# A two-layer hybrid diffusion step: work set into the wait for the experts' token list

## The chip, the core and the metric

The kernel runs on one core of one Trainium2 chip. The metric is the device time of one execution, in microseconds (us). The engines are TensorE (PE; its weight loads are listed apart as PEld), VectorE (DVE), ScalarE (ACT), GpSimd (POOL) and SyncE (SP), which issues most of the transfers. Each engine takes its instructions in the order of its own queue.

## The reference, cut to what matters

```python
for l in range(DEPTH):                                  # 2 layers; 128 context and 512 latent tokens
    mod = jax.nn.silu(cond) @ w_ada[l] + b_ada[l]       # w_ada: (1024, 6144); shift, scale, gate, twice
    shift1, scale1, gate1, shift2, scale2, gate2 = jnp.split(mod, 6, axis=-1)
    u = x * (1 + scale1) + shift1
    ...                                                 # attention, pooling and convolution mixers
    x = layer_norm(ALPHA * x + gate1 * mix, ln1_g, ln1_b)
    u = x * (1 + scale2) + shift2
    x = layer_norm(ALPHA * x + gate2 * expert_choice_ffn(u, ...), ln2_g, ln2_b)

def expert_choice_ffn(u, w_router, w_gate, w_up, w_down):
    cap = CAPACITY_FACTOR * T // N_EXPERTS              # 64 latent tokens, 16 context tokens an expert
    aff = jax.nn.softmax(u @ w_router, axis=-1)
    g, idx = lax.top_k(aff.swapaxes(1, 2), cap)         # each of 16 experts picks its tokens
    xs = jax.vmap(lambda ub, ib: ub[ib])(u, idx)
    hdn = jax.nn.silu(xs @ w_gate) * (xs @ w_up)        # (1024, 512) an expert
    ye = (hdn @ w_down) * g[..., None]                  # (512, 1024) an expert
    return scatter_add(idx, ye)
```

## The kernel before

Both layers run through the same code: token mixing (`token_mixing`), output projection and routing (`out_proj`), experts (`experts`). A scheduler orders each engine's instructions; `issue_after` sets one behind another, and `mm` and `turn1` (helper `inline`, L239) keep TensorE's instructions in the order in which they are written.

The experts are taken in eight pairs (`j`). A pair has 12 weight tiles of 1 MiB: gate, up and down, for two experts, in halves. `eload` puts them into a ring of 16 places, 5 in `raw` and 11 in `ex`. Places 0 to 11 hold the first pair. Place 12 takes a gate tile of the second pair early; the loads of places 13 to 15 (`GATE`) are held behind a 1x1 memset on POOL which follows the first gather, so that these loads don't meet that gather.

The latent tokens' list comes last before the experts: eight rounds of `topk` on VectorE, some small operations (`route_lat`), a transpose on TensorE (`tcol` of `ldup`, into `ps_tc`), casts to indices (`lgi`). With `lgi`, POOL gathers the first pair's rows (`xsl` from `zrow`); TensorE transposes them (`tr`) and starts the first pair's gate product, `ps_g`. A second transpose (`lvd`) brings the list's weights `lg`.

While the list is made, TensorE does the first pair's context products (`fill`, into `ps_gc`). The rest of the context work of that pair stands behind the list: silu on ACT (`sc`) and product on VectorE (`hc`, L1165), transposes (`ps_hcT`), copy (`hcT`), down products (`ps_dc`, 16 matmuls, which the trace counts as 32), scaling (`yc`), and two scatters on POOL into `yaccc`. Each later pair runs its half latent products, its context products (8 steps `k`), the other half, and the down products.

The modulation `mod` is 6 groups of 2048 columns over the two layers, each in eight blocks (`ada_load`, `ada_compute`: 1 MiB of weights and 4 matmuls a block, L185). The blocks of the second layer's group 1 are the late ones of the first layer: `tick()` sets them among the value projection and the first attention heads. POOL also does the residual rows: `xa` times `ln_g`, plus `ln_b`, then a store into `yacc` (`residual`).

## Time and profile before

| | |
|---|---|
| three runs, median | 1258.03 us (1255.51 to 1258.26) |
| profiled execution, its own time | 1255.77 us |
| its span, first to last instruction | 1254.0 us |
| busy share of the span | PE 94%, PEld 56%, DVE 42%, ACT 29%, POOL 20% |
| bytes moved | 342.34 MB, 273 GB/s over the span |
| first layer: list transposed, first gate product | 361.20 us, 372.38 us |
| second layer: the same | 948.77 us, 959.72 us |

The profiled execution is one of those at the lower end: its own time is 2.26 us under the median. Times inside it are counted from the span's start. A matmul of these weights stands as two records in the trace.

### The profile page before, as it was taken

The numbers are of one execution on the slowest core, as the hardware profiler recorded it, in microseconds if no ns is written. First come the engines' busy times: TensorE is split into PE (matmuls) and PEld (weight loads), VectorE is DVE, ScalarE is ACT, GpSimd is POOL, SyncE is SP. The second block draws the span as 40 slices with busy tenths as digits, with TensorE's granted clock in tenths as the row PEclk, the third lists the DMA queues.
The fourth block names the chain that finished last, engine by engine and source line by source line (L and its number), as shares of the span: only waits on it lengthen the run. The fifth ranks groups of instructions, "written<-read, shape, count | busy, mean of one in ns | idle before, by whom it ended". The sixth has DMA issues, their size and how long they took to land.

```text
span 1254.0 us, 18189 instructions
## 1 busy us (share of the span) xinstructions
PE 1178.4 (94%) x7244; PEld 707.5 (56%) x7244; DVE 523.4 (42%) x1237; ACT 367.8 (29%) x805; POOL 254.6 (20%) x237
## 2 busy tenths in 40 slices
PE   5999999999959999999999999999996999999994
PEld 1887786987723333333359998698762333333331
DVE  1455454775551121111165766477744111111126
ACT  1542234673321111111065324476341111111111
POOL 0210001003341111113134600200334121112304
PEclk8899999999979999999999999999998999999997
DMA  9958674344869999999951414616396999999972
GB/s 366 323 199 318 218 270 168 136 153 148 300 243 405 397 404 400 407 413 373 339 162 66 131 56 201 220 51 221 134 356 234 403 395 406 409 408 400 351 253 84
DMA packets 85077, 342.34 MB, mean 273 GB/s; under 512 B 18712, under 2 KB 32088, under 8 KB 54400
## 3 DMA queue, kind: packets, MB, share of 16 engines
q1 hardware_dynamic: 73568, 305.96, 62.8%
q0 software_dynamic: 9840, 29.45, 8.6%
q10 hardware_dynamic: 1584, 5.77, 1.1%
q8 instruction: 57, 0.93, 0.3%
q14 instruction: 28, 0.23, 0.1%
HBM read 313.73 MB, written 27.51 MB: 272 GB/s over the span
## 4 chain that ended last, share of the span: by engine, by line
PE 85%; DVE 6%; ACT 3%; DMA 2%; issue 2%; POOL 1%; SPq 1%; POOLq 0%; ACTq 0%; DVEq 0%
PE ps_d L239 9%; PE ps_g L239 9%; PE ps_u L239 9%; PE ps_gc L239 8%; PE ps_dc L239 4%; PE ps_ada L185 4%; PE ps_c L230 3%; PE ps_o L230 3%; PE ps_o L231 3%; PE ps_o L232 3%; PE ps_c L231 3%; PE ps_c L232 3%; PE tr L239 1%; PE ps_p L732 1%; PE ps_a L230 1%
## 5 line engine op out<-in xcount | busy, mean ns | idle before, releaser
L239 PE MATMUL ps_d<-wd,hT 128*64 128x512 f32 x512 | 114.4, 596 | 4.8 <-DVE yc L1186 3.2
L239 PE MATMUL ps_g<-wg,xT 128*64 128x512 f32 x512 | 116.1, 595 | 0.1
L239 PE MATMUL ps_u<-wu,xT 128*64 128x512 f32 x512 | 115.4, 592 | 0.0
L239 PE MATMUL ps_gc<-wu,xc 128*32 128x512 f32 x512 | 115.0, 594 | 0.0
L239 PE MATMUL ps_gc<-wg,xc 128*32 128x512 f32 x512 | 115.0, 594 | 0.0
L1163 ACT ACTIVATE sc<-ps_gc 32x512 f32<-32x512 f32 x32 | 18.8, 588 | 304.7 <-PE ps_gc L239 276.3
L1165 DVE TENSOR_TENSOR hc<-ps_gc,sc 32x512 f32<-32x512 f32 x32 | 22.0, 687 | 175.0 <-ACT sc L1163 174.9
L239 PEld LDWEIGHTS ps_d<-wd,hT 128*64 128x64 f32 x512 | 37.0, 137 | 80.2 <-issue 76.1
L239 PEld LDWEIGHTS ps_g<-wg,xT 128*64 128x64 f32 x512 | 36.0, 137 | 75.2 <-issue 70.1
L239 PEld LDWEIGHTS ps_u<-wu,xT 128*64 128x64 f32 x512 | 37.2, 137 | 72.6 <-issue 72.6
L239 PEld LDWEIGHTS ps_gc<-wg,xc 128*32 128x32 f32 x512 | 29.2, 110 | 75.0 <-issue 74.0
L1214 DVE SCALAR_TENSOR_TENSOR ye<-ps_d,lg,gl 128x512 f32<-128x512 f32 x32 | 24.0, 751 | 99.2 <-PE ps_d L239 93.5
L185 PE MATMUL ps_ada<-wada,cs 128*32 128x512 f32 x368 | 58.8, 627 | 5.7 <-DMA wada<-in_w_ada_dram 5.7
L239 PE MATMUL ps_dc<-wd,hcT 128*32 128x512 f32 x512 | 61.2, 621 | 0.9 <-ACT hcT L1174 0.9
L1112 POOL DMA_INDIRECT yaccc<-yc,csi x28 | 39.7, 1419 | 103.3 <-DVE yc L1186 75.9
L1193 DVE TENSOR_TENSOR h<-ps_u,sg 128x512 f32<-128x512 f32 x16 | 11.1, 692 | 104.4 <-PE ps_u L239 104.4
L960 POOL DMA_INDIRECT xsl<-zrow,lgi x16 | 15.9, 992 | 167.5 <-PE tr L239 153.0
L284 POOL TENSOR_TENSOR bsd<-bsd,neg_half 128x1 f32<-128x1 f32 x18 | 11.2, 622 | 134.7 <-DVE bsd L283 134.7
L261 ACT ACTIVATE xT<-tr,modB,modA 128x128 f32<-128x128 f32 x64 | 27.8, 457 | 27.2 <-DVE xT L264 26.9
L1112 POOL DMA_INDIRECT yacc<-ye,lgi x14 | 19.9, 1419 | 78.5 <-DVE ye L1214 46.6
L239 PEld LDWEIGHTS ps_dc<-wd,hcT 128*32 128x32 f32 x512 | 15.4, 114 | 34.8 <-issue 32.0
L227 POOL TENSOR_TENSOR wo00l<-r_wo,wo00h 128x1024 fp32r<-128x1024 f32 x4 | 10.4, 2612 | 114.0 <-ACT wo00h L226 114.0
(616 smaller groups left out, 2808.7 us busy)
## 6 DMA issues: line engine op xcount, KB each, us to landing
wg<-in_w_gate_dram SPq DMA_DIRECT2D x64, 1024.0 KB, 18.4
wu<-in_w_up_dram SPq DMA_DIRECT2D x64, 1024.0 KB, 21.5
wd<-in_w_down_dram SPq DMA_DIRECT2D x64, 1024.0 KB, 22.2
wada<-in_w_ada_dram SPq DMA_DIRECT2D x46, 1024.0 KB, 7.6
r_wo<-in_w_out_dram SPq DMA_DIRECT2D x8, 1024.0 KB, 8.4
zrow<-xa ACTq DMA_DIRECT2D x8, 512.0 KB, 6.0
yacc<-xa POOLq DMA_DIRECT2D x8, 512.0 KB, 8.0
z<-yacc SPq DMA_DIRECT2D x8, 512.0 KB, 8.1
```

The source lines that it names most:

```text
L185: nc.tensor.matmul(ps[32 * j:32 * j + 32, :], lhsT=cs[:, k, :], rhs=w[:, j * 512:(j + 1) * 512], start=(k == 0), stop=(k == KD - 1))
L230: nc.tensor.matmul(out, lhsT=lh, rhs=rh, start=first, stop=False)
L231: nc.tensor.matmul(out, lhsT=lh, rhs=rl, start=False, stop=False)
L232: nc.tensor.matmul(out, lhsT=ll, rhs=rh, start=False, stop=last)
L239: line["pe"] = op(*args, **kw)
L261: nc.scalar.activation(out=out[:, kk, :], in_=ps[:, kk, :], func=AF.Identity, scale=A[:, r, k:k + 1], bias=B[:, r, k:k + 1])
L732: nc.tensor.transpose(pt[:, kk, i * P:(i + 1) * P], prs[i][:, (k0 + kk) * P:(k0 + kk + 1) * P], ident)
L960: ins = nc.gpsimd.indirect_dma_start(out=x, out_offset=None, in_=src, in_offset=bass.IndirectOffsetOnAxis(ap=idx, axis=0))
L1112: nc.gpsimd.indirect_dma_start(out=acc[:, :], out_offset=bass.IndirectOffsetOnAxis(ap=idx[h][0:64, j:j + 1], axis=0), in_=y[hs], in_offset ...
L1163: nc.scalar.activation(out=sc[64 * i + 32:64 * i + 64], in_=pc[64 * i:64 * i + 32], func=AF.Silu)
L1165: nc.vector.tensor_tensor(out=hc[32 * i:32 * i + 32], in0=pc[64 * i + 32:64 * i + 64], in1=sc[64 * i + 32:64 * i + 64], op=ALU.mult)
L1214: order["ye"] = nc.vector.scalar_tensor_tensor(out=ye[:, hs], in0=pd, scalar=lg[:, j:j + 1], in1=gl2[:, hs], op0=ALU.mult, op1=ALU.mult)
```

## The change

Four things move. The first pair's product of silu and up rows goes from VectorE to POOL, with the up rows copied out by ACT (`uc`), and stands ahead of the list. Its down products are split: half of them (`ctx_sums` over f = 0, 1) ahead of the list's transpose, half behind it. In the first layer four of the eight late modulation blocks take ring places 12 to 15 and are multiplied around the list (`ada(0)` to `ada(3)`); the second pair's tiles follow them in those places, behind the gather. In the second layer places 12 to 15 hold second-pair weights, loaded without the hold, and the first two steps of the second pair's context products (`NAHEAD`) are done behind the list. Which bank of `ps_gu` each product takes is now named.

```diff
+        k0 = NSPARE if (l, g) == (1, 1) else 0
+        if k == k0:
+            ada_ps[l, g] = pmisc(f"ps_ada{l}_{g}")
+        ada_mms(l, g, k, k == k0, k == KD - 1)
...
-        def route_late(fill):
+        def route_late(fill, down):
 
 
             ins = turn(3, 1, fill(2), lambda ins: fill(1, ins))
             route(3, fill(1, ins))
             fill(9, order["weighed"])
-            latr = route_lat(rt, rx, topk(rx, afl, CAPL, "ta"))
+            best = topk(rx, afl, CAPL, "ta")
+            sums, rest = down()
+            latr = route_lat(rt, rx, best, rest)
             order.pop("gather", None)
             x_first = gather(newrow("xsl"), zrow[:, :], latr[0][:, 0:1])
             cpool(f"rx{l}")
-            return latr, x_first
+            return latr, x_first, sums
         return A, B, ctxr, ln, gates, newrow, newhalf, residual, xc, route_late, ps_dn
 
...
         nc.vector.tensor_copy(out=dup, in_=idf.rearrange("e (o s) -> e o s", o=1).to_broadcast([NE, 2, CAPL]))
-        ps = tcol(dup.rearrange("e o s -> e (o s)"), P)
+        ps = tcol(dup.rearrange("e o s -> e (o s)"), P, turn1)
         order["listed"] = order["tcol"]
+        between()
...
         vd = rx.tile([NE, 2, CAPL], F32, tag="rep", name="lvd")
         nc.vector.tensor_copy(out=vd, in_=vals.rearrange("e (o s) -> e o s", o=1).to_broadcast([NE, 2, CAPL]))
-        ps = tcol(vd.rearrange("e o s -> e (o s)"), P)
...
         nslot, paced = [0], []
+        spare = NSPARE if l + 1 < a["depth"] else 0
+        gate = NEX + NRAW if spare else NE * 6
         line.clear()
 
         def eload(src, shape, name):
 
             n = nslot[0]
-            i = n % (NEX + NRAW)
+            i = (n if n < NEX + NRAW else n - spare) % (NEX + NRAW)
             nslot[0] += 1
             if i < NRAW:
                 t = raw.tile(shape, F32, tag="raw", name=name, bufs=NRAW)
             else:
                 t = ex[EXORDER[i - NRAW]].tile(shape, F32, tag="ex", name=name)
-            if n == GATE:
+            if n == gate:
                 with tc.issue_after(order["gather"].ins):
-                    nc.gpsimd.memset(t[0:1, 0, 0:1], 0.0)
-            after = behind if n == GATE else order["gated"] if GATE < n < 16 else None
+                    nc.gpsimd.memset(t[(slice(0, 1), *[0] * (len(shape) - 2), slice(0, 1))], 0.0)
+            after = behind if n in (GATE, gate) else order["gated"] if gate < n < gate + 4 else None
             with tc.issue_after(after.ins) if after else ExitStack():
                 ins = nc.sync.dma_start(out=t, in_=src)
             paced.append(ins.ins)
             order["eload"] = ins
-            if n >= PACED:
+            if n >= PACED + spare:
                 tc.add_manual_dep(ins.ins, paced[n - PACE].name,
                                   mybir.DependencyInfo(mybir.DependencyClass.Sync, mybir.DependencyReason.DATA), reason="pace")
-            if n == GATE:
+            if n == gate:
                 order["gated"] = ins
...
         for j in range(NPAIR):
             es = (2 * j, 2 * j + 1)
-            w = {}
+            w = w_next
             for nms in ("gu", "d"):
...
+                pc = ps_gu.tile("ps_gc", 0)
             else:
-                pc, pg, pu = [ps_gu.tile(n) for n in ("ps_gc", "ps_g", "ps_u")]
+                pg, pu = ps_gu.tile("ps_g", 2), ps_gu.tile("ps_u", 0)
...
                 return ins
 
-            def ctx_hidden(after=None):
+            def ctx_hidden(pool=False):
                 sc = newhalf("sc")
                 hc = newhalf("hc")[0:64]
+                uc = newhalf("uc") if pool else pc
                 for i in range(2):
-                    nc.scalar.activation(out=sc[64 * i + 32:64 * i + 64], in_=pc[64 * i:64 * i + 32], func=AF.Silu)
-                    with tc.issue_after(after.ins) if after else ExitStack():
-                        nc.vector.tensor_tensor(out=hc[32 * i:32 * i + 32], in0=pc[64 * i + 32:64 * i + 64],
-                                                in1=sc[64 * i + 32:64 * i + 64], op=ALU.mult)
+                    up = slice(64 * i + 32, 64 * i + 64)
+                    nc.scalar.activation(out=sc[up], in_=pc[64 * i:64 * i + 32], func=AF.Silu)
+                    if pool:
+                        nc.scalar.copy(out=uc[up], in_=pc[up])
+                    (nc.gpsimd if pool else nc.vector).tensor_tensor(out=hc[32 * i:32 * i + 32], in0=uc[up], in1=sc[up], op=ALU.mult)
...
 
             def ctx_rows(hcT, pd=None):
-                if pd is None:
-                    pd = ps_dn.tile("ps_dc")
-                for f in range(4):
+                return ctx_scaled(ctx_sums(hcT, pd or ps_dn.tile("ps_dc")))
+
+            def ctx_sums(hcT, pd, fs=range(4)):
+                for f in fs:
                     for q in range(4):
                         i, n = q // 2, q % 2
                         mm(pd[32 * q:32 * q + 32, :], lhsT=hcT[:, f, 32 * i:32 * i + 32],
                            rhs=w["d", i, f // 2][:, f % 2, n * 512:n * 512 + 512], start=(f == 0), stop=(f == 3))
+                return pd
+
...
                         return context(ks)
 
-                (lgi, lso, lg, llast), x_first = route_late(fill)
+                pc_next = ps_gu.tile("ps_gc", 1)
+
+                if spare:
+                    for k in range(spare):
+                        ada_load(1, 1, k, eload)
+                    ada_ps[1, 1] = ps_gu.tile("ps_adae", 2)
+                else:
+                    for nm in "gu":
+                        for i in range(2):
+                            w_next[nm, i, 0] = eweight(nm, 2 + i, 0)
+
+                def ada(k):
+                    if spare:
+                        ada_mms(1, 1, k, k == 0, k == spare - 1, mm)
+
+                def down():
+
+                    warm = st([P, 1], "warm")
+                    with tc.issue_after(order["weighed"].ins):
+                        nc.scalar.activation(out=warm, in_=neg_half, func=AF.Silu)
+                    hc = ctx_hidden(True)
+                    ada(0)
+                    ada(1)
+                    hcT = ctx_turn(hc)
+                    ada(2)
+                    pd = ctx_sums(hcT, ps_dn.tile("ps_dc"), range(2))
+                    return pd, lambda: ctx_sums(hcT, pd, range(2, 4))
+
+                (lgi, lso, lg, llast), x_first, pd = route_late(fill, down)
+                if spare:
+                    ada(3)
+                    ada_sum = st([P, 512], "adao", bufs=1)
+                    nc.scalar.copy(out=ada_sum, in_=ada_ps.pop((1, 1)))
+                    ada_store(1, 1, ada_sum)
+                else:
+                    context(range(NAHEAD), pc_next, w_next, (2, 3))
+                pg, pu = ps_gu.tile("ps_g", 2), ps_gu.tile("ps_u", 0)
                 xp = opool(f"xT{l}", "left")
-                scatter(yaccc, ctx_rows(ctx_turn(ctx_hidden(order["lgi"]))), csi, j)
+                with tc.issue_after(order["lgi"].ins):
+                    yc = ctx_scaled(pd)
+                scatter(yaccc, yc, csi, j)
                 xs0 = load_x(0)
...
     depth = a["depth"]
     ada_todo = [(l, g, k) for l, g in ((0, 1), (0, 2), (1, 0)) for k in range(KD) if l < depth]
-    ada_late = [[(1, g, k) for k in range(KD)] if depth > 1 else [] for g in (1, 2)]
+    ada_late = [[(1, g, k) for k in range(k0, KD)] if depth > 1 else [] for g, k0 in ((1, NSPARE), (2, 0))]
 
```

TensorE's queue in the first layer, from the last context product to the first gate product (`ps_adae` are the moved blocks; names end in a layer, an index and a buffer number). Before:

```order
L239 MATMUL ps_gc<-wu_1_1_3597,xc_2870 32x512
L988 MATMUL ps_tc<-ident,ldup 128x16
L988 MATMUL ps_tc<-ident,lvd 128x16
L239 MATMUL ps_hcT<-ident,hc 128x64 x4
L239 MATMUL ps_dc<-wd_0_0_3599,hcT 32x512 x2
```

In the changed kernel:

```order
L250 MATMUL ps_gc<-wu_1_1_3573,xc_2846 32x512
L250 MATMUL ps_adae<-wada_1_0_3587,cs 32x512 x4
L250 MATMUL ps_adae<-wada_1_1_3589,cs 32x512 x4
L250 MATMUL ps_hcT<-ident,hc 128x64 x4
L250 MATMUL ps_adae<-wada_1_2_3591,cs 32x512 x4
L250 MATMUL ps_dc<-wd_0_0_3575,hcT 32x512 x2
L250 MATMUL ps_dc<-wd_1_0_3577,hcT 32x512 x2
L250 MATMUL ps_dc<-wd_0_0_3575,hcT 32x512 x2
L250 MATMUL ps_dc<-wd_1_0_3577,hcT 32x512 x2
L250 MATMUL ps_tc<-ident,ldup 128x16
L250 MATMUL ps_dc<-wd_0_1_3579,hcT 32x512 x2
```

The third modulation block and half of the down products now stand ahead of the list's transpose; the other half, the second transpose and the fourth block stand between it and `tr`.

SP's queue in the first layer, the last loads before the list. Before:

```order
L1076 DMA wd_0_0_3599<-in_w_down_dram 128x2048
L1076 DMA wd_1_0_3601<-in_w_down_dram 128x2048
L1076 DMA wg_2_0_3883<-in_w_gate_dram 128x2048
L1076 DMA wd_0_1_3603<-in_w_down_dram 128x2048
L1076 DMA wd_1_1_3605<-in_w_down_dram 128x2048
L222 DMA gl_0_3607<-modd_93 128x1024
```

In the changed kernel:

```order
L1092 DMA wd_0_0_3575<-in_w_down_dram 128x2048
L1092 DMA wd_1_0_3577<-in_w_down_dram 128x2048
L1092 DMA wada_1_0_3587<-in_w_ada_dram 128x2048
L1092 DMA wada_1_1_3589<-in_w_ada_dram 128x2048
L1092 DMA wd_0_1_3579<-in_w_down_dram 128x2048
L1092 DMA wd_1_1_3581<-in_w_down_dram 128x2048
L233 DMA gl_0_3583<-modd_93 128x1024
L1092 DMA wada_1_2_3591<-in_w_ada_dram 128x2048
L1092 DMA wada_1_3_3593<-in_w_ada_dram 128x2048
```

One tile less of the second pair and four blocks more stand there; the third and fourth block come last.

POOL's queue in the second layer, around the first gather (`xsl`). Before:

```order
L336 TENSOR_TENSOR xa<-xa,ln_g_7846 128x1024
L337 TENSOR_TENSOR xa<-xa,ln_b_7849 128x1024
L960 DMA xsl<-zrow,lgi 128x1024
L336 TENSOR_TENSOR xa<-xa,ln_g_7846 128x1024
L960 DMA xsl<-zrow,lgi 128x1024
L1073 MEMSET wg_3_0_8856 1x1
```

In the changed kernel:

```order
L1187 TENSOR_TENSOR hc<-uc,sc 32x512 x2
L1128 DMA yaccc<-yc,csi_8114 384x512
L347 TENSOR_TENSOR xa<-xa,ln_g_7856 128x1024
L973 DMA xsl<-zrow,lgi 128x1024
L347 TENSOR_TENSOR xa<-xa,ln_g_7856 128x1024
L973 DMA xsl<-zrow,lgi 128x1024
L1128 DMA yaccc<-yc,csi_8115 384x512
```

The first scatter of `yc` and a residual product stand ahead of the gather now. In the first layer POOL's queue has the two `hc` and one residual product ahead of the gather, and the scatter behind the second gather.

## Rows read from the trace of the kernel before

**Rows 1.** Timeline of TensorE (PE), first layer: start, length, instruction, idle before it.
```profile
352.73 0.59 PE L239 MATMUL ps_gc<-wu,xc 128*32 128x512 f32 x1
361.20 0.28 PE L988 MATMUL ps_tc<-ident,ldup 16*128 16x16 f32 x1 [7.88 <-DVE ldup L1035]
...
364.74 0.71 PE L239 MATMUL ps_hcT<-ident,hc 64*128 64x64 f32 x4 [1.81 <-DVE hc L1165]
365.92 5.26 PE L239 MATMUL ps_dc<-wd,hcT 128*32 128x512 f32 x32 [0.46 <-ACT hcT L1174]
371.11 1.24 PE L239 MATMUL tr<-ident,xsl 128*128 128x128 f32 x8
372.38 3.65 PE L239 MATMUL ps_g<-wg,xT 128*64 128x512 f32 x16
```

**Rows 2.** Timeline of VectorE (DVE), first layer, around the list.
```profile
361.52 0.34 DVE L1040 CAST lgi<-ps_tc 64x8 int32<-64x8 f32 x2 [0.38 <-PE ps_tc L988]
...
371.26 0.75 DVE L1186 SCALAR_TENSOR_TENSOR yc<-ps_dc,cg,gc 128x512 f32<-128x512 f32 x1 [6.66 <-PE ps_dc L239]
```

**Rows 3.** Timeline of POOL, first layer, around the list.
```profile
350.54 2.39 POOL L336 TENSOR_TENSOR xa<-xa,ln_g 128x1024 f32<-128x1024 f32 x1 [7.83 <-DMA zrow<-xa]
...
362.14 1.05 POOL L960 DMA_INDIRECT xsl<-zrow,lgi  x1 [6.79 <-DVE lgi L1040]
...
372.30 1.54 POOL L1112 DMA_INDIRECT yaccc<-yc,csi  x1 [1.67 <-DVE yc L1186]
```

**Rows 4.** Timeline of all engines, second layer, around the list.
```profile
948.77 0.28 PE L988 MATMUL ps_tc<-ident,ldup 16*128 16x16 f32 x1 [7.88 <-DVE ldup L1035]
...
949.71 1.04 POOL L960 DMA_INDIRECT xsl<-zrow,lgi  x1 [5.62 <-DVE lgi L1040]
...
959.72 3.65 PE L239 MATMUL ps_g<-wg,xT 128*64 128x512 f32 x16
```

**Rows 5.** Gathers' DMA issues by stretch (361:363, 949:951, 953:955): median us to landing last.
```profile
xsl<-zrow,lgi POOLq DMA_INDIRECT x1, 4.2
...
xsl<-zrow,lgi POOLq DMA_INDIRECT x1, 4.3
...
xsl<-zrow,lgi POOLq DMA_INDIRECT x1, 9.4
```

**Rows 6.** Stretches: length, busy of PE, PEld, DVE, ACT, POOL, then PEclk, DMA share, GB/s.
```profile
349.00:353.00 4.00, 3.53 (x33) 1.02 (x33) 3.49 (x14) 1.25 (x1) 2.39 (x1) 1.00 1.00 418
353.00:357.00 4.00, 0.32 (x4) 0.00 (x0) 3.86 (x18) 0.59 (x1) 2.34 (x1) 0.82 0.27 111
...
365.00:369.00 4.00, 3.54 (x20) 1.06 (x23) 0.00 (x0) 0.37 (x1) 3.83 (x5) 0.50 0.60 207
...
945.00:949.00 4.00, 0.23 (x1) 0.18 (x1) 3.49 (x16) 0.00 (x0) 0.00 (x0) 0.64 0.00 0
```

**Rows 7.** Groups by line and form: busy us, mean ns of one | idle before.
```profile
L1469 POOL TENSOR_TENSOR z<-z,ln_g 128x384 f32<-128x384 f32 x3 | 3.6, 1190 | 4.6 <-ACT z L1461 4.6
...
L1163 ACT ACTIVATE sc<-ps_gc 32x512 f32<-32x512 f32 x32 | 18.8, 588 | 304.7 <-PE ps_gc L239 276.3 <-DVE hc L1165 28.3
```

**Rows 8.** The chain that ended last: start, length, piece (x counts trace records).
```profile
194.43 1.00 PE ps_ada L185 x8
...
402.70 7.00 PE ps_gc L239 x64
```

**Rows 9.** Start of the first layer's attention: timelines of PE, DVE and ACT.
```profile
211.62 3.63 PE L185 MATMUL ps_ada<-wada,cs 128*32 128x512 f32 x30
...
216.95 0.82 DVE L675 TENSOR_REDUCE mx<-sc 128x1 f32<-128x640 f32 x1 [0.66 <-PE sc L692]
...
218.04 1.28 ACT L678 ACT_TABLE_LOAD   x1 [3.32 <-DVE mx L676]
```

**Rows 10.** Two tiles' instructions on DVE: duration ns min/median/max, first and last start.
```profile
L227 DVE TENSOR_TENSOR ml<-mixC,mh x10: 677/685/1531, 214.8 to 903.2; 128x512 fp32r<-128x512 f32 x10
...
L975 DVE MAX8 tav<-affl x8: 398/400/421, 350.1 to 945.1; 48x8 f32<-48x256 f32 x8
```

More of the change, by code (lines that the diff above doesn't have):

```diff
@@ L46 @@
 NRAW = 5
+NSPARE = 4
+NAHEAD = 2
 NEX = 11
@@ L101, in __init__, with tile @@
             self.shape, self.turn = list(shape), 0
-        def tile(self, name):
+        def tile(self, name, at=None):
+            if at is not None:
+                self.turn = at
             pool = self.pools[self.turn % len(self.pools)]
@@ L177, in ada_load, with ada_mms, ada_store, ada_compute @@
         ada_w[l, g, k] = load(a["w_ada"][l][:, cols].rearrange("(p k) n -> p k n", k=KD)[:, k, :], [P, 2048], f"wada{l}_{g}_{k}")
-    def ada_compute(l, g, k):
-        if k == 0:
-            ada_ps[l, g] = pmisc(f"ps_ada{l}_{g}")
+    def ada_mms(l, g, k, first, last, put=nc.tensor.matmul):
         w, ps = ada_w.pop((l, g, k)), ada_ps[l, g]
         for j in range(4):
-            nc.tensor.matmul(ps[32 * j:32 * j + 32, :], lhsT=cs[:, k, :],
-                             rhs=w[:, j * 512:(j + 1) * 512], start=(k == 0), stop=(k == KD - 1))
+            put(ps[32 * j:32 * j + 32, :], lhsT=cs[:, k, :], rhs=w[:, j * 512:(j + 1) * 512], start=first, stop=last)
+    def ada_store(l, g, o):
+        for r in range(2):
+            dst = modd[l][r:r + 1, g * 2048:(g + 1) * 2048].rearrange("r (j n) -> (r j) n", j=4)
+            nc.gpsimd.dma_start(out=dst, in_=o[r:P:32, :], accum_op=ALU.add)
+    def ada_compute(l, g, k):
+        k0 = NSPARE if (l, g) == (1, 1) else 0
+        if k == k0:
+            ada_ps[l, g] = pmisc(f"ps_ada{l}_{g}")
+        ada_mms(l, g, k, k == k0, k == KD - 1)
         if k == KD - 1:
             o = st([P, 512], "adao", bufs=1)
-            nc.vector.tensor_copy(out=o, in_=ps)
+            nc.vector.tensor_copy(out=o, in_=ada_ps[l, g])
             if (l, g) == (0, 0):
                 return o
-            for r in range(2):
-                dst = modd[l][r:r + 1, g * 2048:(g + 1) * 2048].rearrange("r (j n) -> (r j) n", j=4)
-                nc.gpsimd.dma_start(out=dst, in_=o[r:P:32, :], accum_op=ALU.add)
+            ada_store(l, g, o)
     def load_pk(out, src):
@@ L983, in topk, with tcol @@
         return vals, idf
-    def tcol(src, rows):
+    def tcol(src, rows, put=nc.tensor.transpose):
         ps = pmisc("ps_tc")[0:rows, 0:NE]
-        order["tcol"] = nc.tensor.transpose(ps, src, ident[0:NE, 0:NE])
+        order["tcol"] = put(ps, src, ident[0:NE, 0:NE])
         return ps
@@ L1020, in route_ctx, with route_lat @@
         return gi, si, g, clast
-    def route_lat(rt, rx, best):
+    def route_lat(rt, rx, best, between):
         va, ia = [x[0:NE] for x in best]
@@ L1048, in route_lat @@
         nc.vector.tensor_copy(out=vd, in_=vals.rearrange("e (o s) -> e o s", o=1).to_broadcast([NE, 2, CAPL]))
-        ps = tcol(vd.rearrange("e o s -> e (o s)"), P)
+        ps = tcol(vd.rearrange("e o s -> e (o s)"), P, turn1)
         g = rt.tile([P, NPAIR], F32, name="lg")
@@ L1121, in load_z @@
             return z
-        behind = order["store"]
+        behind, w_next = order["store"], {}
         for j in range(NPAIR):
             es = (2 * j, 2 * j + 1)
-            w = {}
+            w = w_next
             for nms in ("gu", "d"):
@@ L1130, in experts @@
                         for i, e in enumerate(es):
-                            w[nm, i, g] = eweight(nm, e, g)
+                            if (nm, i, g) not in w:
+                                w[nm, i, g] = eweight(nm, e, g)
+            w_next = {}
             if j == 0:
@@ L1137, in experts @@
                 LDQ.dma_start(out=hot[:, 0:TL], in_=a["k_iota"].partition_broadcast(P))
-            if j:
-                pg, pu, pc = [ps_gu.tile(n) for n in ("ps_g", "ps_u", "ps_gc")]
-            else:
-                pc, pg, pu = [ps_gu.tile(n) for n in ("ps_gc", "ps_g", "ps_u")]
+            if j == 0:
+                pc = ps_gu.tile("ps_gc", 0)
+            else:
+                pg, pu = ps_gu.tile("ps_g", 2), ps_gu.tile("ps_u", 0)
+                pc = pc_next if j == 1 else ps_gu.tile("ps_gc", 1)
             def lat(hf):
@@ L1148, in lat, with context @@
                                rhs=w[nm, i, hf][:, k % 4, :], start=(k == 0), stop=(k == KD - 1))
-            def context(ks):
+            def context(ks, pc=pc, w=w, es=es):
                 for k in ks:
@@ L1244, in experts @@
                 lat(0)
-                context(range(KD))
+                context(range(NAHEAD if j == 1 and not spare else 0, KD))
                 hc = ctx_hidden()
@@ L1306, in join @@
             return res
+        ps_gu.turn = 2
         joined = [join(t) for t in range(2)]
```

1 line of the change is left out of this document (added).

## The prediction

> **What bounds the kernel now.** The page gives TensorE 94% of the span, so only its remaining waits can be won, and I looked for those around the list. The timeline of TensorE [rows 1] shows, in the first layer, the last context product ending at 353.32 (352.73 + 0.59), then a wait of 7.88 us for `ldup`: VectorE is finding the latent tokens. From the list's transpose at 361.20 it takes another 11.18 us to the first gate product at 372.38. The second layer repeats this: the same 7.88, then 10.95 us from 948.77 to 959.72 [rows 4]. From the gate product on TensorE works almost without a gap, so **the time of that product in each layer is what the change can move**, less any work that was behind it and is now done ahead.
>
> What ends those 11 us? POOL starts the gather 0.94 us after the list's transpose, at 362.14 [rows 3]; its landing takes 4.2 us from there [rows 5], so the rows are in SBUF at 366.3. Yet `tr` starts at 371.11: until 371.18 TensorE is busy with the context rows' transposes and down products [rows 1], which wait for `hc` behind the list. They are also slow: 16 down products, 32 records, take 5.26 us, where 64 records of such products take 7.00 at full clock [rows 8], so 3.50 for 32. The windows [rows 6] say why: the granted clock is 0.50 at 365 to 369, after the long wait. Losing 5.26 - 3.50 = 1.76 us at half rate means 3.52 us of it at half rate, up to 369.44, or **4.7 us after TensorE's work resumed** at 364.74. I use that below.
>
> **First layer.** Ahead of the list come now silu, copy and product, then transposes and half of the sums.
> - *Product ready.* One silu of 32x512 takes 0.59 [rows 7]; I take the PSUM copy `uc` as the same. No POOL product of 512 columns is in the trace: 384 columns cost 1.19 [rows 7] and 1024 cost 2.39 [rows 3], and the line through both gives 1.43. From 353.4: silu, copy, then two products behind one another, the last waiting for the second copy at 355.8 and the first product at 356.0: ready at 357.5. Transposes and their copy took 1.18 (364.74 to 365.92 [rows 1]); the down products could start at 358.8.
> - *But the third block stands ahead of them on TensorE, and its weights come late.* The transfers run at 418 GB/s until 353 and move 111 GB/s x 4 us after it, which is 1.06 us at full rate: they end at 354.06 [rows 6]. Four blocks for one tile are 3 MiB more, 3.15 MB / 418 GB/s = 7.5 us: they end at 361.6, and the third of four 2.5 us earlier, at 359.1. Then come the block (1.00 [rows 8]) and half of the sums, 16 records or 1.75: list transposed at 361.85 at full clock, 364.6 if all runs at half clock. I take 363.0, since TensorE will have waited, with little between, from about 355.
> - *Then.* Gather 0.94 later, landing 4.2, and 1.27 from `tr` to the gate product: 363.0 + 6.4 = 369.4. The other half of the sums, the second transpose and the fourth block (1.75, 0.3, 1.00) lie inside the 5.1 us until the rows land. The first scatter, behind the second gather on POOL, no longer precedes anything TensorE waits for. **Gain 372.4 - 369.4 = 3.0**, between 1.4 (list at 364.6) and 4.1 (361.85).
>
> **The first layer's attention.** Four blocks leave TensorE here. Some 3.6 us of them (30 records) ran at 211.62, straight ahead of the first scores [rows 9]. That is no gain by itself: the exponentials wait 3.32 us for VectorE's `mx`. VectorE is held by `ml`, which starts at 214.8 whatever the scores do and takes 1.53 instead of 0.69 [rows 10]. With the scores earlier, both reductions (0.82 each [rows 9]) stand ready behind it and go ahead of the small scalar operation: 214.8 + 1.53 + 1.64 = 218.0, and then that operation, for the first exponential's table load, against 218.04. So 0 here; -1 if the longer pause lowers the clock, +3.6 if `ml` came earlier too. What hides the removed blocks is thus that VectorE work.
>
> **Second layer.** Here no blocks stand in the way and half of the sums fit before the list (from 945 TensorE is idle [rows 6]); even at half clock they delay it by little: list at 949.3, against 948.77. The loss is behind it, **in POOL's queue**. It is in order, and the first scatter and a residual product now precede the gather. The scatter waits for `yc`, and `yc` for all 16 down products. Step by step: second half of the sums until 951.1, `yc` 0.75 [rows 2] until 951.9, 0.29 to the scatter (372.01 to 372.30 [rows 2, 3]), scatter 1.54 until 953.8, product 2.39 until 956.2 [rows 3], gather at 956.25 instead of 949.71. With its landing of 4.3 [rows 5] and 1.27: gate product at 961.8, **2.1 later** than 959.72.
> TensorE fills part of that pause with two context steps of the second pair, 2/8 of 7.00 = **1.75 that is then saved** [rows 8]. They end at about 953; the next work is at 960.6, after a wait as long as those that dropped the clock to 0.50. If it again takes 4.7 us from there to return, half of it is lost: **2.3**. Together 2.1 + 2.3 - 1.75 = 2.6 lost. Ends: 0 if the clock stays up and the list is as early as before; 5.6 if the list comes 1 us late and the gather's landing is 2 us longer beside the scatter.
>
> **Parts at nothing.** Warm-up activations stand at the head of ScalarE's queue, long before they could matter; the bank order changes no wait. In the second layer the 3 MiB loaded without the hold come while TensorE is the bound, and end before the gather; in the first, the second pair's tiles come behind the gather, and are wanted some 20 us later. Residual sums and stores come up to 10 us later, hidden behind the first pair's products; without that cover it would be their 2.39 each.
>
> **Sum.** 3.0 + 0 - 2.6 = 0.4 faster: 1255.4 against the profiled execution's own 1255.77. The median of the runs is 2.26 higher, so against it 1257.6. A change under 0.2%, 2.5 us, can't be told from none.
>
> **The rivals.**
> *(a) Faster: the second layer loses nothing.* If TensorE's clock is back sooner or POOL reaches its gather earlier, the 1.75 saved pays for the 2.1, and with the first layer at its good end the net is 4 us: 1254. For it: the clock stood at 0.82 and 0.64 within these waits [rows 6], so it doesn't fall at once. Against: it was 0.50 right after both. If the attention also gains its 3.6, 1250.4; the row of `mx` speaks against that.
> *(b) Slower: the gather behind the scatter lands late.* The one gather in the trace that went out amid other traffic took 9.4 us, not 4.3 [rows 5]. The scatter goes out 2.4 us ahead of it. At 9.4 the gate product is 5.1 later: net 4.7 lost, 1262.7. It decides for slower from a landing of about 7.2 on (0.4 - 2.9 = -2.5). Against: in this layer all tiles have landed by then, and the first gathers of both layers landed in 4.2 to 4.3.
> *(c) VectorE and POOL hold each other up.* `ml` beside a POOL product took 1531 ns instead of 685, `tav` beside POOL at most 421 instead of 400 [rows 10]. POOL's `hc` and its residual product now run until about 359.9, where before its busy time in this wait ended with 2.34 us between 353 and 357 [rows 6]. The list's last small operations lie just before 361.20; the worst is a wait behind one product, 2.39: first layer's gain 0.6, net 2.0 slower, 1260.0. Mostly not, as the transpose waits for the sums anyway. The Trainium skill, SBUF — State Buffer, section "SBUF: two separate sides", says that an operation of VectorE with two SBUF inputs and one of GpSimd exclude one another for a whole instruction. The row of `ml` agrees, that of `tav` (one input) too; by that rule (c) is the full price, and the sum would be 1260.0.
>
> **How the numbers follow.** Forecast, between 1255 and 1260: 0.50. (a) 0.22, with the attention's gain 0.05 more; (b) 0.18; (c) 0.05, at the edge of what can be told. Faster is 0.27; slower is (b) and a part of (c), 0.21; 0.52 remains. The likeliest case's own range is 1255 to 1260; reaching to (a) and nearly to all of (b) gives 1252.5 to 1262.
>
> **What the changed kernel's profile would show.** In the first layer TensorE waiting on a transfer ahead of the third block near 359; the list's transpose near 363 and the gate product near 369.4. If that transpose waits for `ldup` and not for TensorE's own queue, the third block was not late. In the second, POOL's gather near 956, behind scatter and product; its landing separates (b) from the forecast, the granted clock of the gate product separates (a). I am wrong if the gather stands near 950 there, or if the first exponential moves away from 218.

## The result, and the profile after

The changed kernel takes 1277.03 us (median of 4 runs, 1274.39 to 1278.32) against 1256.94 for the kernel before: ratio 1.0152, interval 1.0138 to 1.0167, so 20 us **slower** where 0.4 faster was forecast. Its profiled execution has a span of 1275.9 us, 21.9 more; it lies 0.7 above its median, the profiled one of the kernel before 1.2 below. How far like events lie behind those of the kernel before tells where they went:

| event | before | changed | behind |
|---|---|---|---|
| first exponential's table load, first layer | 218.04 | 222.52 | 4.48 |
| first layer: last context product ends | 353.32 | 357.83 | 4.51 |
| first layer: first gate product | 372.38 | 376.86 | 4.48 |
| first layer: first `ps_z`, after the last pair | 628.78 | 644.86 | 16.08 |
| second layer: last context product ends | 940.89 | 957.12 | 16.23 |
| second layer: first gate product | 959.72 | 980.46 | 20.74 |
| second layer: first `ps_z` | 1216.68 | 1238.36 | 21.68 |

Three steps: 4.5 us at the attention, 11.6 among the first layer's experts, 4.5 at the second layer's list. The first layer's list, where 3.0 were to be won, moves nothing.

**The attention.** Timelines of POOL, VectorE and ScalarE of the changed kernel (start, length, instruction, idle before it), to be held against [rows 9, 10]:

```profile
213.99 1.71 POOL L192 DMA_DIRECT2D modd<-adao  x2 [40.24 <-DVE adao L202]
215.12 5.24 POOL L238 TENSOR_TENSOR wo00l<-r_wo,wo00h 128x1024 fp32r<-128x1024 f32 x2
215.03 5.89 DVE L238 TENSOR_TENSOR ml<-mixC,mh 128x512 fp32r<-128x512 f32 x1 [0.73 <-ACT mh L237]
220.84 1.54 DVE L686 TENSOR_REDUCE mx<-sc 128x1 f32<-128x640 f32 x2
222.52 1.28 ACT L689 ACT_TABLE_LOAD   x1 [7.53 <-DVE mx L687]
```

`ml` ends only when both of POOL's products (215.12 to 220.36) have ended, after 5.89 us. In the kernel before the same products ran from 213.35 to 218.54, and `ml` was done at 216.29, in 1.53. They now come later because the sum of the modulation blocks is complete four blocks sooner, and its store stands ahead of them on POOL.

**The first layer's list.** TensorE's timeline, to be held against [rows 1]:

```profile
357.65 1.90 PE L250 MATMUL ps_adae<-wada,cs 128*32 128x512 f32 x16
361.85 0.69 PE L250 MATMUL ps_hcT<-ident,hc 64*128 64x64 f32 x4 [2.30 <-POOL hc L1187]
365.70 1.94 PE L250 MATMUL ps_adae<-wada,cs 128*32 128x512 f32 x8 [3.16 <-DMA wada<-in_w_ada_dram]
367.41 2.81 PE L250 MATMUL ps_dc<-wd,hcT 128*32 128x512 f32 x16
370.15 0.23 PE L250 MATMUL ps_tc<-ident,ldup 16*128 16x16 f32 x1
370.31 1.92 PE L250 MATMUL ps_dc<-wd,hcT 128*32 128x512 f32 x16
375.38 1.55 PE L250 MATMUL tr<-ident,xsl 128*128 128x128 f32 x8 [1.99 <-DMA xsl<-zrow,lgi]
376.86 4.94 PE L250 MATMUL ps_g<-wg,xT 128*64 128x512 f32 x16
```

TensorE waits for the third block's weights; the block and most of the sums run at half rate (granted clock 0.58 from 365 to 370); the list stands 12.32 us after the last context product instead of 7.88, and the gate product 19.03 instead of 19.06. That product now itself begins at half clock: 4.94 for 3.65.

**The first layer's last pair.** TensorE's timeline again; the kernel before has no such waits:

```profile
620.05 3.65 PE L250 MATMUL ps_u<-wu,xT 128*64 128x512 f32 x14 [3.03 <-DMA wu<-in_w_up_dram]
...
632.27 1.04 PE L250 MATMUL ps_d<-wd,hT 128*64 128x512 f32 x2 [1.47 <-DMA wd<-in_w_down_dram]
635.15 7.06 PE L250 MATMUL ps_d<-wd,hT 128*64 128x512 f32 x22 [1.84 <-DMA wd<-in_w_down_dram]
644.86 1.13 PE L250 MATMUL ps_z<-z,ident 128*128 128x512 f32 x2
```

Why weights, 245 us after the change? The memset on POOL that releases the held loads, before and changed:

```profile
366.72 0.09 POOL L1073 MEMSET wg<- 1x1 f32 x1
375.64 0.09 POOL L1089 MEMSET wg<- 1x1 f32 x1
```

The windows of the kernel before, then of the changed one (columns as in [rows 6]; the last two are the transfers' share and GB/s):

```profile
360.00:365.00 5.00, 0.80 (x4) 0.64 (x5) 3.67 (x16) 0.59 (x1) 2.82 (x2) 0.50 0.22 39
365.00:370.00 5.00, 4.54 (x28) 1.30 (x31) 0.00 (x0) 0.37 (x1) 4.60 (x5) 0.58 0.60 202
370.00:375.00 5.00, 4.97 (x32) 2.08 (x26) 2.30 (x5) 2.89 (x5) 2.11 (x2) 1.00 1.01 406
...
450.00:500.00 50.00, 50.00 (x308) 18.17 (x306) 11.89 (x27) 6.49 (x15) 8.04 (x6) 1.00 1.02 403
```

```profile
365.00:370.00 5.00, 4.30 (x24) 0.98 (x24) 0.57 (x4) 0.00 (x0) 0.00 (x0) 0.58 0.25 102
370.00:375.00 5.00, 3.39 (x30) 0.84 (x26) 1.91 (x9) 0.59 (x1) 3.75 (x3) 1.00 0.34 105
375.00:380.00 5.00, 4.62 (x18) 2.16 (x20) 1.55 (x4) 2.53 (x5) 4.82 (x6) 0.66 0.75 235
...
450.00:500.00 50.00, 50.00 (x306) 18.08 (x304) 12.29 (x28) 7.82 (x17) 7.65 (x6) 1.00 1.02 410
```

Among the experts the transfers are as full as TensorE, at some 400 GB/s, in both kernels. The memset stands 8.9 us later, 4.4 against the gate product; and one tile more lies behind it, 1 MiB or 2.6 us at that rate. By this sum the last tile is 7.0 us late; TensorE waits 6.34 in all. Of the 11.6 us, 1.3 are the slow first gate product; what is left over goes with a lower clock around these waits (0.83 granted at 630 to 640).

**The second layer's list.** TensorE, then POOL, to be held against [rows 4]:

```profile
961.14 0.74 PE L250 MATMUL ps_hcT<-ident,hc 64*128 64x64 f32 x4 [4.02 <-POOL hc L1187]
962.34 3.64 PE L250 MATMUL ps_dc<-wd,hcT 128*32 128x512 f32 x16 [0.46 <-ACT hcT L1195]
965.91 0.28 PE L250 MATMUL ps_tc<-ident,ldup 16*128 16x16 f32 x1
978.55 1.98 PE L250 MATMUL tr<-ident,xsl 128*128 128x128 f32 x8 [8.29 <-DMA xsl<-zrow,lgi]
980.46 5.21 PE L250 MATMUL ps_g<-wg,xT 128*64 128x512 f32 x16
...
969.86 1.55 POOL L1128 DMA_INDIRECT yaccc<-yc,csi  x1 [8.77 <-issue]
971.48 2.33 POOL L347 TENSOR_TENSOR xa<-xa,ln_g 128x1024 f32<-128x1024 f32 x1
973.98 1.02 POOL L973 DMA_INDIRECT xsl<-zrow,lgi  x1 [0.17 <-issue]
```

As forecast, scatter and residual product go first, and the gather leaves 8.07 us after the list.

### The profile page after: what moved, and what is told of

It is laid out like the page before. It is cut to its first block, busy times and chain, and to the rows that moved or that the text cites. A ratio compares the mean times of both kernels' runs of the same rounds, so it can differ in the third digit from the quotient of the medians.

```text
span 1275.9 us, 18200 instructions
## 1 busy us (share of the span) xinstructions
PE 1187.7 (93%) x7244; PEld 708.8 (56%) x7244; DVE 524.8 (41%) x1233; ACT 371.9 (29%) x812; POOL 261.3 (20%) x242
## 5 line engine op out<-in xcount | busy, mean ns | idle before, releaser
L250 PE MATMUL ps_d<-wd,hT 128*64 128x512 f32 x512 | 117.9, 603 | 8.6 <-DMA wd<-in_w_down_dram 3.9
L250 PE MATMUL ps_g<-wg,xT 128*64 128x512 f32 x512 | 118.9, 607 | 0.0
L1187 DVE TENSOR_TENSOR hc<-ps_gc,sc 32x512 f32<-32x512 f32 x28 | 19.2, 687 | 172.7 <-ACT sc L1184 172.7
L187 PE MATMUL ps_ada<-wada,cs 128*32 128x512 f32 x336 | 55.5, 634 | 4.7 <-DMA wada<-in_w_ada_dram 4.7
L275 DVE TENSOR_SCALAR xT<-tr,modA,modB 128x128 f32<-128x128 f32 x64 | 25.0, 408 | 28.8 <-PE tr L250 20.3
```

The lines of the kernel that those rows point to most:

```text
L187: put(ps[32 * j:32 * j + 32, :], lhsT=cs[:, k, :], rhs=w[:, j * 512:(j + 1) * 512], start=first, stop=last)
L250: line["pe"] = op(*args, **kw)
L275: nc.vector.tensor_scalar(out=out[:, kk, :], in0=ps[:, kk, :], scalar1=A[:, r, k:k + 1], scalar2=B[:, r, k:k + 1], op0=ALU.mult, op1=ALU.add)
L1187: (nc.gpsimd if pool else nc.vector).tensor_tensor(out=hc[32 * i:32 * i + 32], in0=uc[up], in1=sc[up], op=ALU.mult)
```

## The experiments

All are the changed kernel with one edit, unless said otherwise. "Stretch" is the time from the first layer's first gate product to its first `ps_z`: 256.40 us before, 268.00 changed.

**e1, the store behind POOL's products**

```diff
-            ada_store(l, g, o)
...
+        with tc.issue_after(order["split"].ins):
+            ada_store(1, 1, order.pop("late"))
```

> The changed kernel, with the store of the modulation sum (modd<-adao) put behind POOL's wo00l products instead of ahead of them. Theory: the store delays wo00l, so that ml on VectorE meets both POOL products and takes 5.89 us; with the store behind, ml takes about 1.5 as before, the first exponential's table load stands near 218 instead of 222.5, and the time falls by 4 to 4.5 us to about 1272.6. The wait for weights in the first layer's last pair stays near 10 us, since everything before it shifts by the same. Rival: the stall comes from the four blocks that are gone from TensorE's queue or from its clock; then ml, the table load and the time stay as they are (1277).

Measured: 1273.05, ratio 1.0124 (1.0103 to 1.0144). POOL, VectorE and ScalarE:

```profile
214.20 5.16 POOL L241 TENSOR_TENSOR wo00l<-r_wo,wo00h 128x1024 fp32r<-128x1024 f32 x2 [39.86 <-ACT wo00h L240]
215.61 1.55 DVE L241 TENSOR_TENSOR ml<-mixC,mh 128x512 fp32r<-128x512 f32 x1 [0.73 <-ACT mh L240]
218.76 1.28 ACT L695 ACT_TABLE_LOAD   x1 [3.19 <-DVE mx L693]
```

4.0 less. One store's place on POOL made the stall. At the last context product (355.00) 2.8 of the 4.5 us are back. The stretch stays: 267.88.

**e2, the gather first**

```diff
-                scatter(yaccc, yc, csi, j)
+                with tc.issue_after(order["gather"].ins):
+                    scatter(yaccc, yc, csi, j)
```

> The changed kernel, with the first scatter held behind the first gather on POOL. Theory: in the second layer the gather goes out 1 us after the list (near 967 instead of 974), the gate product comes 7 us earlier and, after a shorter wait, at a higher clock: 7 to 8.5 us less, about 1269. The first layer doesn't change, as its scatter was behind the gather already. Rival: the second layer loses by the list, which waits for the down products at half clock, and not by POOL's queue; then at most 1.5 us (the scatter's own length) come back, about 1275.5.

Measured: 1266.63, ratio 1.0087 (1.0059 to 1.0115), 10.4 less. TensorE in the second layer:

```profile
962.76 0.23 PE L250 MATMUL ps_tc<-ident,ldup 16*128 16x16 f32 x1
...
968.10 1.23 PE L250 MATMUL tr<-ident,xsl 128*128 128x128 f32 x8 [1.24 <-DMA xsl<-zrow,lgi]
```

The gather leaves at 963.66, the gate product follows at 969.35 in 3.65 us, at full clock: 15.30 after the last context product instead of 23.34. The whole of 8 us is POOL's queue. The rest of the fall is a shorter stretch, 263.96, which this edit doesn't explain: e1 has 267.88 and e7 264.69 with the same list and the same hold, so the stretch differs by some 4 us without a cause that these runs show.

**e3, no blocks moved**

```diff
-NSPARE = 4
+NSPARE = 0
```

> The changed kernel with no modulation block moved: all eight stay ahead of the attention, and the first layer does what the second does (second pair's tiles in the last places, loaded without the hold, two context steps behind the list). Theory: the attention's stall goes, the wait for the first layer's last weights goes, since 16 expert tiles instead of 12 are loaded ahead of the list and 80 instead of 84 behind; each layer keeps the second layer's loss of about 4.4: 1257 + 2 x 4.4 = 1266. Rival for the last weights: they come late by the ring's order or pacing and not by the amount of transfer that is left; then about 10 us more, 1276.

Measured: 1265.61, ratio 1.0074 (1.0053 to 1.0095). No wait for weights, stretch 256.18; the first layer's gate product 23.17 after its last context product, as the second's in the changed kernel. The time is as expected, in part by luck: the first layer's last context product ends at 356.01, 2.7 us later than before, and that was not foreseen. Ahead of the list ScalarE's copy of the routing sums (`parts`) waits 2.78 us, which the trace puts to a `wd` load, and the third store of `zrow` leaves at 345.09 instead of 342.65. No run tests this.

**e4, loads not held**

```diff
-        gate = NEX + NRAW if spare else NE * 6
+        gate = NE * 6 + spare
```

> The changed kernel, where the first layer's second-pair tiles follow the modulation blocks in places 12 to 15 without being held behind the first gather. Theory (the transfers set the pace of the first layer's experts, and their idle time from 365 to 376 is what the last pair waits for): two of them start as soon as the first two blocks are multiplied, near 365, the last pair's wait of 10 us falls below 5; against that the first gather lands amid traffic, in about 9 instead of 4.3 us, so that the first gate product comes up to 5 later. Time 1272 to 1277. Rival: the last pair's wait has to do with the order of the ring; then it stays near 10 us and the time rises to about 1281.

Measured: 1270.23, ratio 1.0106 (1.0085 to 1.0128). Better than the range expected. The last pair's waits are gone and the stretch is 258.44, although the first gate product is slower still (5.73). The transfers no longer pause (windows of 365 to 380):

```profile
365.00:370.00 5.00, 5.00 (x29) 1.31 (x33) 2.10 (x9) 0.00 (x0) 0.67 (x1) 0.66 1.01 416
370.00:375.00 5.00, 2.65 (x25) 0.55 (x17) 1.60 (x8) 0.59 (x1) 4.48 (x4) 1.00 0.98 390
375.00:380.00 5.00, 3.77 (x14) 2.21 (x16) 1.55 (x4) 1.62 (x4) 4.82 (x5) 0.55 0.95 368
```

The gather amid this traffic brought its rows 5.9 us after its start (370.30 to 376.23), not 9.

**e5, the third block behind the list** (and e2's edit, and the sum's store behind the gather)

```diff
-                    ada(2)
                     pd = ctx_sums(hcT, ps_dn.tile("ps_dc"), range(2))
...
                 if spare:
+                    ada(2)
                     ada(3)
```

> As e2_gather_first, and in the first layer the third modulation block stands behind the list with the fourth, instead of ahead of the down products; the sum's store and the first scatter are held behind the first gather. Theory: the list no longer waits for the third block's weights; it is transposed 8.7 us after the last context product, as in the second layer, instead of 12.2, the gate product follows 15.5 instead of 19.1 after it and at full clock, and the time falls by 3.5 to 5 us against e2, to about 1262. The last pair's wait stays, since gather and held loads move by the same. Rival: the blocks behind the list delay the gathered rows' transposes instead; then the gate product stays at 19 and the time at 1266.6.

Measured: 1269.20, ratio 1.0095 (1.0075 to 1.0115): a miss in time. The list stands 8.60 after the last context product and the gate product 15.63, at full clock, as expected; so the third block was what held the list. But the stretch grew to 271.96. POOL's queue in e5:

```profile
373.09 1.86 POOL L192 DMA_DIRECT2D modd<-adao  x2 [3.12 <-ACT adao L1284]
...
380.34 0.09 POOL L1089 MEMSET wg<- 1x1 f32 x1
```

The store, which waits 3.12 us for the sum, and the first scatter stand ahead of the memset by this edit, so that the held loads are released at 380.34, 11.4 us after the gather; in e2 it was 4.6. What TensorE won, it waited for in weights: 6.3 us in the first layer, from 411 us on, against 4.1 in e2.

**e6, the kernel before with one tile more held**

```diff
-GATE = 13
+GATE = 12
```

> The kernel before, with one tile more held behind the first gather (places 12 to 15 instead of 13 to 15), in both layers: nothing but 1 MiB of weights, 2.6 us of transfer, moves behind the list. Theory (the kernel before has hardly any slack there: in the changed kernel the held loads start 4.4 us later against the gate product and are 1 MiB more, 7.0 us in all, and TensorE waits 6.3, so the slack is about 0.7): TensorE waits about 1.9 us for the first layer's last weights, and with the clock after it the time rises by 2 to 4 us; in the second layer nothing or as much again. Rival: the transfers have several us of slack in the kernel before, and the changed kernel's wait has another cause; then no wait for weights and no change (within 1 us).

Measured: 1258.78, ratio 1.0014 (1.0004 to 1.0023), 1.8 us by the ratio. The profiled execution has waits of 0.34 and 1.41 us for the first layer's last down tiles and of 2.17 in the second; less than the 2.6 us that were moved, by 0.9 and 0.4. But it is the slowest of the twelve (1262.55). The median lost 1.8 for both layers, a little less than expected, so in most executions the slack is somewhat more: 1.7 us a layer, if each lost half (an estimate). By the same sum the changed kernel had 0.7 (7.0 late, 6.34 waited), and e2 2.7 (6.8 late, 4.08 waited). So there is little slack, but not none.

**e7, `ml` first** (its half of `mix_split` is written ahead of `wo00`'s split; POOL's queue stays as it was)

```diff
-        w2 = [wout_split(l, raws[0], 0, 0, nc.gpsimd)]
+        w2 = [wout_tiles(l, 0, 0)]
...
+        mixed[CTX] = mix_half(ms, mixC, CTX)
+        wout_split(l, raws[0], 0, 0, nc.gpsimd, w2[0], order["split"])
```

> The changed kernel, with ml of the convolution's half written ahead of the wo00 split and POOL's wo00l products held behind it, so that ml meets no POOL product. Theory (VectorE's ml, which reads two operands, stands still while POOL's product runs): ml takes 0.7 us instead of 5.89, the first exponential's table load follows the first scores, near 216 instead of 222.5, and the time falls by 6 to 7 us to about 1270.5. Rival: ml is slow by itself or the exponential waits for something else; then the load stays within 1 us of 222.5.

Measured: 1270.28, ratio 1.0110 (1.0094 to 1.0127), 6.8 less. The table load stands at 216.05. POOL and VectorE:

```profile
215.28 5.26 POOL L239 TENSOR_TENSOR wo00l<-r_wo,wo00h 128x1024 fp32r<-128x1024 f32 x2
214.37 0.68 DVE L239 TENSOR_TENSOR ml<-mixC,mh 128x512 fp32r<-128x512 f32 x1
...
216.26 0.82 DVE L690 TENSOR_REDUCE mx<-sc 128x1 f32<-128x640 f32 x1 [0.30 <-PE sc L707]
...
218.46 2.44 DVE L698 TENSOR_SCALAR pr<-pr,sm 128x640 f32<-128x640 f32 x1
```

Ahead of the product `ml` takes 0.68. `mx`, which reads PSUM, runs undisturbed beside it; `pr`, from SBUF to SBUF, takes 2.44 us instead of 0.55 and ends 0.36 after POOL's second product. Of the 6.5 us won at the table load only 3.1 are left at the last context product (354.72): TensorE waits 2.05 us for ScalarE's `pr` (218.28) and 1.90 for VectorE's (220.95), where in the kernel before it had a modulation block (218.31) and waited 0.90 and 0.46, and the granted clock from 220 to 240 is 0.84 for 0.91. The other 3.3 are a shorter stretch, 264.69, as in e2. So the 6.8 agree with the forecast partly by luck.

**e8 and e9, composed:** e2, e3 and e7 with four context steps ahead instead of two; e9 puts two more queue places right, which e8 showed.

```diff
-NAHEAD = 2
+NAHEAD = 4
```

In e9 also (`after` is the first pairs' copy of `hT`, `down_last` the last `ps_d`):

```diff
+                with tc.issue_after(after.ins) if after else ExitStack():
+                    nc.scalar.activation(out=res[n], in_=res[n], func=AF.Copy, scale=ALPHA)
...
+                with tc.issue_after(down_last.ins) if t > 1 else ExitStack():
+                    put(ps, lhsT=ident, rhs=zs[t][:, cols], start=True, stop=False)
```

> Composed of what the runs so far point to: no modulation block moved (as e3), the first scatter behind the first gather (as e2), ml ahead of POOL's wo00l (as e7), and four context steps of the second pair behind the list instead of two. Theory: in each layer the gate product comes 15.3 to 15.8 us after the last context product instead of 18.9 and 3.5 us of context work are done by then: 2 x 6.5 to 7 us; the attention gives 0.5 to 1: about 1243 to 1245, faster than both kernels. Rival: in the first layer 3 MiB more are in transfer while the list is made, the first gather lands in 9 instead of 4.3 us, and the last weights come late again: then the first layer gives nothing, and the time is 1250 or more.

Measured: 1264.12, ratio 1.0059 (1.0041 to 1.0078): a miss. Both gate products come nearly as expected (15.40 and 16.11 after the context products), but TensorE waits 4.28 us for a copy behind `ln_b` on ScalarE (387.63, itself held 6.58 by a load) and 11.77 at the end for `z`, since the `ps_z` of the last tokens had moved ahead of the last pair's down products.

> As e8, with two queues put right: ScalarE's scaling of ln_b, which waits for a late load, no longer stands ahead of the copy of hT in the first pair, and the last tokens' ps_z stays behind the last pair's down products on TensorE. Theory: e8 was 6.6 us ahead of the kernel before at the last pair's up products, although it had lost 5.1 us (4.28 of wait and 1.65 at half clock, against 0.78) at that copy in the first layer; both come through now: 11 to 12 us less than before, about 1246. The first layer's last weights stay in time, as 16 expert tiles are loaded ahead of the list. Rival: the first layer's gain is eaten by waits for weights, since TensorE now runs 6 us ahead of the loads; then such waits appear behind 400 us and the time is 1250 or more.

Measured: 1254.86, ratio 0.9991 (0.9972 to 1.0011): not told from the kernel before. The rival held. TensorE in the first layer's last pair:

```profile
608.82 3.65 PE L251 MATMUL ps_u<-wu,xT 128*64 128x512 f32 x14 [1.58 <-DMA wu<-in_w_up_dram]
...
619.79 1.04 PE L251 MATMUL ps_d<-wd,hT 128*64 128x512 f32 x2 [0.22 <-DMA wd<-in_w_down_dram]
622.21 5.36 PE L251 MATMUL ps_d<-wd,hT 128*64 128x512 f32 x22 [1.37 <-DMA wd<-in_w_down_dram]
630.22 1.12 PE L251 MATMUL ps_z<-z,ident 128*128 128x512 f32 x2
```

The second layer has waits of 0.58 and 1.53 for its last down tiles. The first layer's last context product ends at 355.83, 2.5 us later than before, with the same wait of ScalarE as in e3 (2.69).

**e10, four blocks kept, queues put right** (e5 with the store behind the memset, e7, e8's four steps in the second layer, e9's places)

```diff
+            if j == 1 and "sum" in order:
+                with tc.issue_after(order["hold"].ins):
+                    ada_store(1, 1, order.pop("sum"))
```

> The changed kernel's idea with its queues put right: four modulation blocks stay in places 12 to 15, two ahead of the list and two behind it; the first scatter behind the first gather; the sum's store behind the release of the held loads; ml ahead of POOL's wo00l; four context steps ahead in the second layer; the two queue places of e9. Theory: attention 2 us less than before, second layer 7 less; in the first layer the gate product comes 3.4 earlier, but the held loads start some 7 us later against it than before and are 1 MiB (2.6 us) more, so that TensorE waits 8 to 10 us for the last weights: 2 + 7 + 3.4 - 9 or so: 1252 to 1257. Rival: the transfers catch up during eight pairs; then no such wait and about 1245.

Measured: 1264.65, ratio 1.0065 (1.0047 to 1.0084). Waits of 1.05, 1.32 and 1.76 us in the first layer and of 2.03 in the second, stretch 265.93: as the theory says in kind, but 8 to 13 us more in time, a miss. The attention's 1.5 us (table load at 216.53) were gone again by the first layer's last context product, at 355.36, 2.0 behind the kernel before. The trace has the same waits as e7 beside `pr`, 2.05 and 1.90 us, and a granted clock of 0.83 from 220 to 240.

**e11 and e12, fewer bytes** (e11: e2, with fewer bytes in the first layer and e9's place for `ps_z`; e12: e9, with fewer bytes in both layers)

```diff
-                ins = nc.sync.dma_start(out=t, in_=src)
+                ins = nc.sync.dma_start(out=t[:, 0:part] if part else t, in_=src[:, 0:part] if part else src)
```

> As e2_gather_first, but in the first layer the sixth pair's eight gate and up tiles are loaded by half (its products read the loaded half twice, so that part of the computation is changed): 4 MiB, 10 us of transfer, less in front of the last pair, and the same instructions in the same order on TensorE and POOL. Theory (the first layer's experts wait for the sum of the transfers): no wait for weights at the last pair, and the stretch from the first gate product to the first ps_z of the last tokens falls from 263.96 in e2 to about 257.5 (256.40 in the kernel before, plus 1.2 for a gate product at half clock): 6.3 us less, about 1260.5. Rival (a tile of the last pair comes late by its place in the ring or by a wait of its queue): the waits of 1.37 and 2.33 us stay, and so does the time, 1266.6.

Measured: 1258.69, ratio 1.0018 (1.0003 to 1.0033), 7.9 less than e2. No wait for weights, stretch 257.29. TensorE in the first layer's last pair:

```profile
616.21 3.60 PE L250 MATMUL ps_u<-wu,xT 128*64 128x512 f32 x16
...
624.99 7.09 PE L250 MATMUL ps_d<-wd,hT 128*64 128x512 f32 x32
```

> As e9_composed, with the sixth pair's gate and up tiles loaded by half in both layers (as in e11, the computation is changed there). Theory: e9's queues are right and the transfers alone hold it: its waits of 1.58, 0.22, 1.37, 0.58 and 1.53 us for weights go, with the clock that they cost, 5 to 7 us less than e9: 1248 to 1250. Rival: the transfers cost only what is seen as waits for the late tiles themselves, or something else follows them: 1253 or more.

Measured: 1243.87, ratio 0.9893 (0.9875 to 0.9912), 11 less than e9 and faster than expected. No wait for weights; stretch 252.93, which is 256.40 less four context steps (3.50). So what the queues had won in the stretch was there, and in e9 the transfers took it back. The kernel before wasn't run with fewer bytes; its profile has no wait for weights among the experts that they could take away.

## Why the prediction was wrong

The terms, in us, gains positive:

| term | forecast | measured | by |
|---|---|---|---|
| attention of the first layer | 0 | -4.5 | e1, e7 (2.8 and 3.1 of it) |
| first layer, gate product | +3.0 | 0.0 | e5 |
| first layer, that product at half clock | 0 | -1.3 | its length, 4.94 |
| first layer, weights behind the list | 0 | -10.3 | e4, e6, e11 |
| second layer, list to end | -2.6 | -5.4 | e2 |

The measured terms make 21.5 of the span's 21.9. The page of the kernel before has these rows on the transfers, for 40 slices of 31.35 us:

```profile
DMA  9958674344869999999951414616396999999972
GB/s 366 323 199 318 218 270 168 136 153 148 300 243 405 397 404 400 407 413 373 339 162 66 131 56 201 220 51 221 134 356 234 403 395 406 409 408 400 351 253 84
```

- **Parts at nothing: the failed step.** "in the first, the second pair's tiles come behind the gather, and are wanted some 20 us later." So the late start of the held loads was put at nothing; it cost 10.3 us. In e1, e2 and e7, which leave the first layer's list and hold as they are, the same term is 10.0, 6.4 and 7.1. I asked when the next tiles are wanted, and not what the transfers have to do in all. Among the experts they are as full as TensorE, and the last pair pays for a late start of the first load. The rows above say so (tenths of 9 from 376 to 627, at 397 to 413 GB/s up to 564), and I read the transfers only up to the list. e4 takes away the late start, e11 the amount: the wait goes with either, and e6 shows little slack in the kernel before.
- **The attention.** I left `ml` at the 1.53 of its row, though rival (c) named what governs it, and I followed POOL's queue only at the list. Counting each DMA past which a step moves would have found the store. The price of (c) was one product; `ml` waited for two. The exponential moved away from 218, which the prediction had named as a sign that it was wrong. Taking `ml` out of POOL's way (e1, e7) gives back 2.8 and 3.1 of the 4.5 us at the last context product. For the rest, e7 and e10 show TensorE's waits beside `pr` and a lower clock where the removed blocks had stood; that these are the cause is argued, not tested.
- **First layer.** The mechanism was right; the third block's arrival was mis-sized. I let the blocks land one after another, 2.5 us apart. The transfers ended where they were put, near 361.6 (366 less the 4.5 from the attention), but the third block was usable only at 365.70, when all were about done (the share of 0.25 at 365 to 370 is 1.25 us). Then its block and the first sums ran mostly at half clock, 4.5 us for 2.75. List at 12.3 instead of 9.7 after the last context product.
- **Second layer.** Right in sign, place and order, too small in size: the gate product came 4.5 later, not 2.1. Against the forecast the list was 0.4 later, the gather 1.1 (8.07 after the list for 6.95), its landing 0.3 (4.57 for 4.3), and from `tr` to the gate product it took 0.6 more. The half clock cost 1.56 in the gate product and 0.74 in `tr`: 2.3, as forecast; a wait of 0.63 for a weight at the end is more. Rival (b), a landing of 9.4, didn't come.
- **Rival (c).** The Trainium skill, SBUF — State Buffer, section "SBUF: two separate sides", gives an exclusive lock between POOL's operations and those of VectorE with two SBUF inputs or in a two-port mode, to whichever starts first. The trace agrees in kind: `ml` (two inputs) stands still, `mx` (reading PSUM) doesn't; `pr` takes 2.44 us, but no row shows in which mode it ran. It doesn't agree on who goes first: `ml` stood behind both products although its recorded start is 0.09 us ahead of the first. Why, and why it passes in 1.55 us in e1, no run here shows.

## What to carry to other kernels

Before moving work into a wait, ask which second resource is full in the stage behind it, and how much slack that has to the stage's end: a stage in which TensorE and the transfers are both full gives back, for an earlier start of TensorE alone, little more than that slack. When a sum is ready sooner, look at which queue its store now leads. And a step that is moved ahead of an in-order queue's urgent instruction is priced by all that it waits for itself.

## What was not expected of the hardware

A VectorE operation of 0.69 us took 5.89 beside two POOL products, about four times as long as in the kernel before, because these began 1.8 us later (215.12 for 213.35). Of two tiles issued one behind the other, the first was usable half a microsecond, not 2.5, before the transfers ended. And a gather in the midst of transfers at 390 to 416 GB/s brought its rows in 5.9 us, where [rows 5] had 9.4 for a later one.
